# A hybrid decoder layer on one core: feed-forward features in two halves, the residual stream in DRAM during the mixer, five buffers of split weights, loads of small vectors apart from their use

## The chip, the cores and the metric

The kernel runs on one core of a Trainium2 chip. The metric is device microseconds for one execution of the whole program, as a median of several runs. Beside the timed runs one execution was profiled; its span goes from the first to the last instruction, and every trace row below is from that execution.

## The reference

One decoder layer on x, 256 positions by 2048 features, float32:

```
x = x + 0.5 * swiglu(rms_norm(x, ffn1_norm), ffn1_w_gate, ffn1_w_up, ffn1_w_down)     # 2048 -> 5632 -> 2048
h = rms_norm(x, mix_norm)
proj = h @ w_in                                        # 2048 -> 11776: q, k, v of two attentions, two gates
dq, dk = rope(rms_norm(q)), rope(rms_norm(k))          # per head, 128 wide
o_dil  = dilated attention, 3 head groups x 4 heads, mixed over the groups
o_diff = differential attention, 4 heads: softmax1 - lambda * softmax2, with a norm per head
         lambda = exp(sum(lq1 * lk1)) - exp(sum(lq2 * lk2)) + lam_init
y = sigmoid(g_dil) * (o_dil @ w_dil_branch) + sigmoid(g_diff) * (o_diff @ w_diff_branch)
x = x + y @ w_out
x = x + 0.5 * swiglu(rms_norm(x, ffn2_norm), ffn2_w_gate, ffn2_w_up, ffn2_w_down)

swiglu(h) = (silu(h @ w_gate) * (h @ w_up)) @ w_down
```

## The kernel before, in words

**Every large product goes through `linear` (L99).** It makes a block of 512 output columns for all 256 positions: two tiles of 128 positions (`NT`), each with a PSUM bank of its own. The weights come in groups of two blocks of 128 rows (`GRP`, 512 KB a group). For a group, `weight_groups` (L83) loads the raw float32 rows on SP's queue (`raw`, pool `wraw`, four buffers), ScalarE rounds them to the matmul's type (`w_hi`, L95), and VectorE takes the rest (`w_lo`, L96); these two tiles are in pool `wspl`, with three buffers of each. TensorE then does three products for each block of rows and each position tile: high by high (L111), high by low (L112), low by high (L113). So a group is 12 matmuls of 512 columns. There are 768 groups in the program: 176 for gate and up and 88 for down in each feed-forward, 184 for `w_in`, 24 for the two branches, 32 for `w_out`. A buffer of `w_hi` and `w_lo` comes free when TensorE has finished the group that read it.

**The clock of the program text is the group.** `tick` (L73) counts groups; `defer(n, fn)` (L70) puts a piece of work into the program text n groups later. The order on each engine is then made by the planner of the framework, which plays the program through with its own durations and lets each engine take what is ready, earlier text first; a load without anything to wait for can so move far ahead of its place in the text. On the chip every engine and every queue goes through its list strictly in that order and waits where something is late. `pinned` (L357 to L360) keeps what ScalarE and VectorE do in a deferred piece behind the newest split.

**Feed-forward (`ffn`, L231).** For each of 11 chunks of 512 features: gate (8 groups), SiLU, up (8 groups), product on VectorE (L247). The chunk is then turned so that features lie on partitions: `turn_blocks` (L149) transposes 32 by 32 blocks on VectorE (L155), writes them to DRAM (`blocks`, L157) and reads them back in another order (`moved`, L160), both on SP's queue. Eight groups later in the text (`BLOCK_WAIT`) `split_blocks` (L163) splits the block into `ah` (ScalarE, L128) and `al` (VectorE, L129). After all 11 chunks come four blocks of down, each of 22 groups over all 44 blocks of features. The block of the last chunk is read by groups 21 and 22 of the first of them. In the first feed-forward each finished block goes through `residual` (L254: added to `xs`, turned, split into `xh` and `xl` for the next product), in the second through `finish` (L660: added to `xs` and stored).

**The mixer** takes `w_in` in 23 blocks, with the attention heads as deferred pieces between the groups. `sig` (L597) holds the first gate, 16 KB a partition, last read by `dil_part` (L625) of the fourth block of the branches. `xs`, the residual stream (L184, 16 KB a partition), lies in SBUF throughout; the mixer only uses it in the `residual` of `w_out`.

**Small vectors.** `rotary` (L301) loads the positions on ScalarE's queue and makes the tables at once; `head_gains` (L333) loads eight vectors of 128 on ScalarE's queue, each broadcast to all partitions (64 KB), and makes lambda from four of them at once (`lq`, L338 to L346).

Of the kernel before, what the change touches and what calls it, by code (L numbers as in the profile page):

```python
# [27 lines left out]
LEAD = 56  # L28
BLOCK_WAIT = 8
GRP = 2  # L30
DIL_G, DIL_H = 3, 4
DIFF_H = 4
ROPE = 32
# [15 lines left out]
def hybrid_layer_kernel(ctx: ExitStack, tc: tile.TileContext, a: dict, out: bass.AP):  # L49
# [1 line left out]

    const = ctx.enter_context(tc.tile_pool(name="const", bufs=1))
    small = ctx.enter_context(tc.tile_pool(name="small", bufs=4))
    wraw = ctx.enter_context(tc.tile_pool(name="wraw", bufs=4))
    wspl = ctx.enter_context(tc.tile_pool(name="wspl", bufs=3))
    work = ctx.enter_context(tc.tile_pool(name="work", bufs=1))
    dram = ctx.enter_context(tc.tile_pool(name="dram", bufs=2, space=bass.MemoryType.DRAM))
    ps_mm = ctx.enter_context(tc.tile_pool(name="ps_mm", bufs=4, space=PSUM))
# [122 lines left out]
        return tot  # L181


    xs = const.tile([P, NT, D], F32, name="xs")  # L184
    xv = a["x"][0].rearrange("(t p) d -> p t d", p=P)
    ident = const.tile([P, P], F32, name="ident")
    make_identity(nc, ident)
# [43 lines left out]
    def ffn(wg, wu, wd, norm, done, ahead=None):  # L231
        with tc.tile_pool(name="act", bufs=1) as apool, tc.tile_pool(name="actw", bufs=2) as aw, \
                tc.tile_pool(name="actb", bufs=1) as bp:
            ah = apool.tile([P, KF, S], F32R, name="ah")
            al = apool.tile([P, KF, S], F32R, name="al")
            for j in range(FF // CH):
                ps = linear(wg, j * CH, xh, xl, KD, ahead if j == 0 else None)
                if j == 0:
                    rs = norm()
                sg = []  # L240
                for t in range(NT):
                    s = aw.tile([P, CH], F32, name="sg")
                    nc.scalar.activation(s, ps[t], AF.Silu, scale=rs[t])  # L243
                    sg.append(s)
                ps = linear(wu, j * CH, xh, xl, KD)
                for t in range(NT):
                    nc.vector.scalar_tensor_tensor(sg[t], ps[t], rs[t], sg[t], op0=ALU.mult, op1=ALU.mult)  # L247
                x = turn_blocks(sg, bp)
                defer(BLOCK_WAIT, lambda x=x, j=j: split_blocks(x, ah, al, 4 * j))
            for n in range(D // CH):  # L250
                ps = linear(wd, n * CH, ah, al, KF)
                done(n, ps, bp)

    def residual(n, ps, scale, gains, ss, pool):  # L254

        cols = slice(n * CH, (n + 1) * CH)
        for t in range(NT):
            nc.vector.scalar_tensor_tensor(xs[:, t, cols], ps[t], scale, xs[:, t, cols],
                                           op0=ALU.mult, op1=ALU.add)
        src = [xs[:, t, cols] for t in range(NT)]  # L260

        def turn():
            x = turn_blocks(src, pool)
            defer(BLOCK_WAIT, lambda: split_blocks(x, xh, xl, 4 * n, gains))

        def squares():
            for t in range(NT):
                sum_squares(ss[t], n, src[t])

        if n < D // CH - 1:  # L270
            defer(1, turn)
        else:
            defer(2, lambda: to_kmajor(src, xh, xl, 4 * n, gains))
        defer(3, squares)
# [25 lines left out]

    def rotary():  # L301

        pos = const.tile([P, NT], I32, name="pos")
        with nc.allow_non_contiguous_dma(reason="256 positions"):
            nc.scalar.dma_start(pos, a["positions"].rearrange("b (t p) -> p (b t)", p=P))
        posf = const.tile([P, NT], F32, name="posf")
        nc.vector.tensor_copy(posf, pos)
        freq = const.tile([P, H], F32, name="freq")
        for i, f in enumerate(INV_FREQ):
            nc.vector.memset(freq[:, i:i + 1], f)  # L310
        ang = const.tile([P, NT, H], F32, name="ang")
        turns = const.tile([P, NT, H], F32, name="turns")
        for t in range(NT):
            nc.vector.tensor_scalar(ang[:, t], freq, posf[:, t:t + 1], None, op0=ALU.mult)
        nc.vector.tensor_scalar(turns, ang, 1.0 / (2.0 * math.pi), MAGIC, op0=ALU.mult, op1=ALU.add)
        nc.vector.tensor_scalar(turns, turns, -MAGIC, None, op0=ALU.add)
        for part in (*TWO_PI, TWO_PI_REST):
            nc.vector.scalar_tensor_tensor(ang, turns, -part, ang, op0=ALU.mult, op1=ALU.add)
        aabs = turns
        nc.vector.scalar_tensor_tensor(aabs, ang, -1.0, ang, op0=ALU.mult, op1=ALU.max)  # L320
        hpi = const.tile([P, 1], F32, name="hpi")
        nc.vector.memset(hpi, math.pi / 2.0)
        sh = const.tile([P, NT, H], F32, name="sh")
        chf = const.tile([P, NT, H], F32, name="chf")
        nc.scalar.activation(sh, ang, AF.Sin, scale=0.5)
        nc.scalar.activation(chf, aabs, AF.Sin, scale=-0.5, bias=hpi)
        nc.vector.scalar_tensor_tensor(sinb[:, :, H:], sh, 2.0, chf, op0=ALU.mult, op1=ALU.mult)
        nc.vector.tensor_scalar(sinb[:, :, :H], sinb[:, :, H:], -1.0, None, op0=ALU.mult)
        nc.vector.tensor_tensor(sh, sh, sh, op=ALU.mult)
        for i in range(2):  # L330
            nc.vector.tensor_scalar(cosb[:, :, i * H:(i + 1) * H], sh, -2.0, 1.0, op0=ALU.mult, op1=ALU.add)

    def head_gains():  # L333

        for i, n in enumerate(("dil_q_norm", "dil_k_norm", "diff_q_norm", "diff_k_norm")):
            nc.scalar.dma_start(qkg[:, i], a[n].to_broadcast([P, P]))
        lq = work.tile([P, 4, P], F32, name="junk")
        for i, n in enumerate(("diff_lq1", "diff_lk1", "diff_lq2", "diff_lk2")):  # L338
            nc.scalar.dma_start(lq[:, i], a[n].to_broadcast([P, P]))
        le = const.tile([P, 2], F32, name="le")  # L340
        for i in range(2):
            nc.vector.tensor_tensor(lq[:, 2 * i], lq[:, 2 * i], lq[:, 2 * i + 1], op=ALU.mult)
# [16 lines left out]
    def pinned(fn):  # L359

        with tc.issue_after(last_hi.ins), tc.issue_after(last_lo.ins):
            fn()

    defer(28, lambda: pinned(masks))
    defer(36, lambda: pinned(rotary))
    defer(44, lambda: pinned(head_gains))
    ss = [small.tile([P, D // CH], F32, name="ss4") for _ in range(NT)]
    ffn(a["ffn1_w_gate"][0], a["ffn1_w_up"][0], a["ffn1_w_down"][0], first_norm,
        lambda n, ps, pool: residual(n, ps, 0.5, later_gains[0], ss, pool), lambda g: load_x(g + 1))


    rstd = []
# [2 lines left out]
    o_dq, o_dk, o_dv = 0, 1536, 3072  # L375
    o_fq, o_fk, o_fv = 4608, 5632, 6656
    o_ga, o_gb = 7680, 9728

    mix = ExitStack()
    midc = mix.enter_context(tc.tile_pool(name="midc", bufs=1))  # L380
# [6 lines left out]
    ob_h = midc.tile([P, 2 * DIFF_H, S], F32R, name="ob_h")  # L387
    ob_l = midc.tile([P, 2 * DIFF_H, S], F32R, name="ob_l")

    def qk_chunk(c0, gain, dst, is_key):  # L390


        ps = linear(w_in, c0, xh, xl, KD)
        if not rstd:
            rstd.extend(rsqrt_mean(total(mix_ss[t]), D, 1) for t in range(NT))
        q = midw.tile([P, NT, 4, P], F32, name="q")
# [55 lines left out]
    fk = fp.tile([P, 2, 4, NT, 4, 32], F32, name="fk")  # L452
    fv = fp.tile([P, NT, 2 * P * DIFF_H], F32, name="fv")
    for i in range(2):
        qk_chunk(o_fq + i * CH, 2, fq[:, 4 * i:4 * i + 4], False)
        qk_chunk(o_fk + i * CH, 3, fk[:, i], True)
        v_chunk(o_fv + i * CH, fv, i * CH)

# [156 lines left out]
    for n in range(D // CH):  # L615
# [29 lines left out]

        defer(2, turn_y)
    gpool.__exit__(None, None, None)
    ss = [small.tile([P, D // CH], F32, name="ss4") for _ in range(NT)]
    for n in range(D // CH):
        ps = linear(a["w_out"][0], n * CH, yh, yl, KD)  # L650
# [45 lines left out]
```

## Time and profile before

| | |
|---|---|
| time, median of 3 runs | 2173.26 us (2169.95 to 2179.61) |
| time of the profiled execution | 2174.9 us |
| its span | 2173.1 us |
| mean granted TensorE clock | 0.998 |
| TensorE busy | 2148.0 us (99%) |
| VectorE busy | 1216.5 us (56%) |
| ScalarE busy | 994.6 us (46%) |
| GpSimd busy | 45.1 us (2%) |
| DMA, mean | 208 GB/s |

1.8 us of the profiled execution lie outside its span. A busy TensorE is not one at its peak: the end of a matmul is modelled, and consecutive matmuls overlap, so the distance from start to start says more than the busy share.

### The profile page before, as it was taken

What the parts mean: (1) busy time and instruction counts of PE and PEld (TensorE: products, weight loads), DVE (VectorE), ACT (ScalarE), POOL (GpSimd) and SP (SyncE); (2) the same over time, 40 slices, a digit from 0 to 9 for tenths busy, and PEclk for the clock granted to TensorE, in tenths of its full rate; (3) what the DMA queues carried; (4) which work ended last, traced back from release to release, by engine and by line L of the source; (5) the groups of instructions that cost most, each with busy time, mean ns of one, the idle gap of its engine ahead of it and who ended that gap; (6) DMA issues with size and microseconds to landing.
All of it is one profiled execution on the core that took longest, in us unless ns stands there. A gap on an engine that the chain in (4) does not pass through costs nothing.

```text
span 2173.1 us, 24998 instructions
## 1 busy us (share of the span) xinstructions
PE 2148.0 (99%) x9490; PEld 1765.7 (81%) x9490; DVE 1216.5 (56%) x1440; ACT 994.6 (46%) x1193; POOL 45.1 (2%) x41
## 2 busy tenths in 40 slices
PE   8999999999999999999999999999999999999999
PEld 7878888888888877887878888888888888888887
DVE  5655555555555466776565556665555555554443
ACT  5434444443444445555455444454444444443333
POOL 0000000000000010101100000000000000000000
PEclk9999999999999999999999999999999999999999
DMA  6666666666666666666654566666666666666654
GB/s 231 211 201 215 218 213 221 220 217 210 209 210 199 198 202 204 205 221 208 208 190 159 184 226 214 218 214 213 213 218 210 223 212 212 224 216 207 203 203 141
DMA packets 241437, 452.04 MB, mean 208 GB/s; under 512 B 14322, under 2 KB 38436, under 8 KB 241316
## 3 DMA queue, kind: packets, MB, share of 16 engines
q1 hardware_dynamic: 239792, 449.89, 63.1%
q8 instruction: 74, 1.21, 0.2%
q10 hardware_dynamic: 1524, 0.55, 0.1%
q14 instruction: 47, 0.39, 0.0%
HBM read 426.80 MB, written 23.59 MB: 207 GB/s over the span
## 4 chain that ended last, share of the span: by engine, by line
PE 79%; DMA 10%; DVE 6%; ACT 2%; issue 2%; POOL 1%; SPq 0%; ACTq 0%; DVEq 0%; POOLq 0%
PE mm L112 26%; PE mm L113 26%; PE mm L111 26%; DMA moved<-blocks 4%; DMA blocks<-turned 4%; DVE w_lo L96 3%; ACT w_hi L95 2%; DVE turned L155 1%; POOL rr L122 1%; DMA q<-blocks 1%; DMA raw<-in_w_out_dram 1%; DMA raw<-in_ffn_w_up_dram 0%; DVE q L407 0%; PE s L552 0%; DMA dk<-blocks 0%
## 5 line engine op out<-in xcount | busy, mean ns | idle before, releaser
L96 DVE TENSOR_TENSOR w_lo<-raw,w_hi 128x1024 fp32r<-128x1024 f32 (+1 forms) x769 | 933.0, 1220 | 793.7 <-ACT w_hi L95 792.8
L95 ACT ACTIVATE w_hi<-raw 128x1024 fp32r<-128x1024 f32 (+1 forms) x769 | 808.8, 1058 | 949.5 <-PE mm L113 919.7
L112 PE MATMUL mm<-w_lo,xh 128*128 128x512 f32 x2144 | 843.1, 393 | 8.4 <-DVE w_lo L96 7.9
L113 PE MATMUL mm<-w_hi,xl 128*128 128x512 f32 x2144 | 834.5, 390 | 0.1
L111 PE MATMUL mm<-w_hi,xh 128*128 128x512 f32 x2144 | 759.3, 392 | 0.1
L112 PEld LDWEIGHTS mm<-w_lo,xh 128*128 128x128 f32 x2144 | 403.8, 188 | 99.6 <-DVE w_lo L96 16.6
L111 PEld LDWEIGHTS mm<-w_hi,xh 128*128 128x128 f32 x2144 | 403.0, 188 | 85.6 <-ACT w_hi L95 1.6
L113 PEld LDWEIGHTS mm<-w_hi,xl 128*128 128x128 f32 x2144 | 403.5, 188 | 83.1 <-DVE xl L132 0.5
L112 PE MATMUL mm<-w_lo,ah 128*128 128x512 f32 x704 | 274.5, 390 | 2.6 <-DVE w_lo L96 2.6
L113 PE MATMUL mm<-w_hi,al 128*128 128x512 f32 x704 | 274.0, 389 | 0.0
L111 PE MATMUL mm<-w_hi,ah 128*128 128x512 f32 x704 | 245.7, 389 | 0.1
L112 PEld LDWEIGHTS mm<-w_lo,ah 128*128 128x128 f32 x704 | 132.2, 188 | 32.2 <-DVE w_lo L96 4.7
L111 PEld LDWEIGHTS mm<-w_hi,ah 128*128 128x128 f32 x704 | 131.8, 188 | 28.6 <-ACT w_hi L95 1.1
L113 PEld LDWEIGHTS mm<-w_hi,al 128*128 128x128 f32 x704 | 132.1, 188 | 27.2
L122 POOL TENSOR_TENSOR rr<-rv,mhalf 128x4 f32<-128x4 f32 (+1 forms) x34 | 44.2, 1306 | 1404.6 <-DVE rv L120 1404.5
L129 DVE TENSOR_TENSOR al<-moved,ah 128x512 fp32r<-128x512 f32 x44 | 28.5, 688 | 73.0 <-ACT ah L128 73.0
L128 ACT ACTIVATE ah<-moved 128x512 fp32r<-128x512 f32 x44 | 25.4, 624 | 86.4 <-DMA moved<-blocks 86.4
L112 PE MATMUL mm<-w_lo,yh 128*128 128x512 f32 x128 | 50.2, 392 | 0.7 <-DVE w_lo L96 0.7
L113 PE MATMUL mm<-w_hi,yl 128*128 128x512 f32 x128 | 49.9, 390 | 0.0
L155 DVE STREAM_TRANSPOSE turned<-sg 128x512 f32<-128x512 f32 x44 | 48.4, 1100 | 0.0
L111 PE MATMUL mm<-w_hi,yh 128*128 128x512 f32 x128 | 44.9, 390 | 0.1
L243 ACT ACTIVATE sg<-mm,rr 128x512 f32<-128x512 f32 x44 | 29.8, 689 | 21.5 <-PE mm L113 21.5
(142 smaller groups left out, 733.4 us busy)
## 6 DMA issues: line engine op xcount, KB each, us to landing
raw<-in_w_in_dram SPq DMA_DIRECT2D x184, 512.0 KB, 3.5
raw<-in_ffn_w_up_dram SPq DMA_DIRECT2D x176, 512.0 KB, 4.5
raw<-in_ffn_w_down_dram SPq DMA_DIRECT2D x176, 512.0 KB, 4.4
raw<-in_ffn_w_gate_dram SPq DMA_DIRECT2D x175, 512.0 KB, 4.0
blocks<-turned SPq DMA_DIRECT2D x41, 512.0 KB, 4.4
raw<-in_w_out_dram SPq DMA_DIRECT2D x32, 512.0 KB, 4.5
moved<-blocks SPq DMA_DIRECT2D x31, 512.0 KB, 4.5
raw<-in_w_diff_branch_dram SPq DMA_DIRECT2D x16, 512.0 KB, 4.7
```

The source lines that it names most:

```text
L95: last_hi = nc.scalar.activation(hi[:, ks], raw[:, ks], AF.Copy)
L96: last_lo = nc.vector.tensor_tensor(lo[:, ks], raw[:, ks], hi[:, ks].bitcast(F32), op=ALU.subtract)
L111: nc.tensor.matmul(ps[t], xh[:, k, sl], hi[:, kk], start=k == 0, stop=False)
L112: nc.tensor.matmul(ps[t], xh[:, k, sl], lo[:, kk], start=False, stop=False)
L113: nc.tensor.matmul(ps[t], xl[:, k, sl], hi[:, kk], start=False, stop=k == nk - 1)
L122: nc.gpsimd.tensor_tensor(r, v, mhalf[:, :cols], op=ALU.pow)
L128: nc.scalar.activation(hi, src, AF.Copy)
L129: nc.vector.tensor_tensor(lo, src, hi.bitcast(F32), op=ALU.subtract)
L155: nc.vector.transpose(r[:, :, t], srcs[t].rearrange("p (kt i q) -> p q kt i", i=32, q=4))
L243: nc.scalar.activation(s, ps[t], AF.Silu, scale=rs[t])
```

## The change

- Pool `wspl` gets five buffers of `w_hi` and `w_lo` instead of three; `wraw` stays at four.
- `ffn` does the features in two halves of 6 and 5 chunks. After the first half come four blocks of down of 12 groups, whose results `part` adds to `xs`; after the second half four blocks of 10 groups, with `residual` or `finish` as before. `ah` and `al` are 24 blocks long instead of 44.
- `xs` moves into a pool of its own at the right end of SBUF. In the first feed-forward `residual` also stores each finished block to DRAM (`x_mid`). The first product of the mixer is pulled ahead of the closing of that pool; the mixer's tiles use its place. Before `w_out`, in the place of `sig`, a new `xs` is loaded from `x_mid` in one transfer of 2 MB on SP's queue.
- The loads of the positions and of the eight small vectors move from ScalarE's queue into `table_loads`, on GpSimd's queue, at group 34 of the text and not pinned. `rotary` moves from group 36 to 40, `head_gains` from 44 to 48.

```diff
+RAW_BUFS = 4
+SPL_BUFS = 5
+HALVES = (6, 5)
...
-    wraw = ctx.enter_context(tc.tile_pool(name="wraw", bufs=4))
-    wspl = ctx.enter_context(tc.tile_pool(name="wspl", bufs=3))
+    wraw = ctx.enter_context(tc.tile_pool(name="wraw", bufs=RAW_BUFS))
+    wspl = ctx.enter_context(tc.tile_pool(name="wspl", bufs=SPL_BUFS))
...
-    xs = const.tile([P, NT, D], F32, name="xs")
+    xpool = tc.tile_pool(name="xpool", bufs=1, side="right")
+    xs = xpool.__enter__().tile([P, NT, D], F32, name="xs")
+    x_mid = dram.tile([NT, P, D], F32, name="x_mid", bufs=1)
...
-            ah = apool.tile([P, KF, S], F32R, name="ah")
-            al = apool.tile([P, KF, S], F32R, name="al")
-            for j in range(FF // CH):
...
+            ah = apool.tile([P, 4 * HALVES[0], S], F32R, name="ah")
+            al = apool.tile([P, 4 * HALVES[0], S], F32R, name="al")
+            rs = None
+            j = 0
+            for half, count in enumerate(HALVES):
+                down = wd[j * CH:(j + count) * CH]
+                for i in range(count):
+                    ps = linear(wg, j * CH, xh, xl, KD, ahead if j == 0 else None)
...
+                    x = turn_blocks(sg, bp)
+                    defer(BLOCK_WAIT, lambda x=x, i=i: split_blocks(x, ah, al, 4 * i))
+                    j += 1
+                for n in range(D // CH):
+                    ps = linear(down, n * CH, ah, al, 4 * count)
+                    (done if half else part)(n, ps, bp)
+
+    def part(n, ps, _):
+        cols = slice(n * CH, (n + 1) * CH)
+        for t in range(NT):
+            nc.vector.scalar_tensor_tensor(xs[:, t, cols], ps[t], 0.5, xs[:, t, cols], op0=ALU.mult, op1=ALU.add)
...
+        if keep is not None:
+            nc.sync.dma_start(keep.rearrange("t p d -> p t d")[:, :, cols], xs[:, :, cols])
...
-        pos = const.tile([P, NT], I32, name="pos")
-        with nc.allow_non_contiguous_dma(reason="256 positions"):
-            nc.scalar.dma_start(pos, a["positions"].rearrange("b (t p) -> p (b t)", p=P))
...
-    def head_gains():
+    def table_loads():
 
         for i, n in enumerate(("dil_q_norm", "dil_k_norm", "diff_q_norm", "diff_k_norm")):
-            nc.scalar.dma_start(qkg[:, i], a[n].to_broadcast([P, P]))
+            nc.gpsimd.dma_start(qkg[:, i], a[n].to_broadcast([P, P]))
         lq = work.tile([P, 4, P], F32, name="junk")
         for i, n in enumerate(("diff_lq1", "diff_lk1", "diff_lq2", "diff_lk2")):
-            nc.scalar.dma_start(lq[:, i], a[n].to_broadcast([P, P]))
+            nc.gpsimd.dma_start(lq[:, i], a[n].to_broadcast([P, P]))
+        lam_in.append(lq)
+        with nc.allow_non_contiguous_dma(reason="256 positions"):
+            nc.gpsimd.dma_start(pos, a["positions"].rearrange("b (t p) -> p (b t)", p=P))
+
+    def head_gains():
+        lq = lam_in[0]
...
+    defer(34, table_loads)
     defer(28, lambda: pinned(masks))
-    defer(36, lambda: pinned(rotary))
-    defer(44, lambda: pinned(head_gains))
+    defer(40, lambda: pinned(rotary))
+    defer(48, lambda: pinned(head_gains))
...
-        lambda n, ps, pool: residual(n, ps, 0.5, later_gains[0], ss, pool), lambda g: load_x(g + 1))
+        lambda n, ps, pool: residual(n, ps, 0.5, later_gains[0], ss, pool, x_mid), lambda g: load_x(g + 1))
...
+    first = linear(w_in, o_fq, xh, xl, KD)
+    xpool.__exit__(None, None, None)
...
-        qk_chunk(o_fq + i * CH, 2, fq[:, 4 * i:4 * i + 4], False)
+        qk_chunk(o_fq + i * CH, 2, fq[:, 4 * i:4 * i + 4], False, None if i else first)
...
     gpool.__exit__(None, None, None)
+    xpool = ctx.enter_context(tc.tile_pool(name="xpool2", bufs=1, side="right"))
+    xs = xpool.tile([P, NT, D], F32, name="xs")
+    nc.sync.dma_start(xs, x_mid.rearrange("t p d -> p t d"))
```

## Rows read from the trace of the kernel before

**Rows 1.** The page: busy time of each engine; shares of the chain that ended last.

```profile
PE 2148.0 (99%) x9490; PEld 1765.7 (81%) x9490; DVE 1216.5 (56%) x1440; ACT 994.6 (46%) x1193; POOL 45.1 (2%) x41
...
PE 79%; DMA 10%; DVE 6%; ACT 2%; issue 2%; POOL 1%; SPq 0%; ACTq 0%; DVEq 0%; POOLq 0%
```

**Rows 2.** Waits of TensorE: waited for, us in total, times, longest us.

```profile
PE mm L112 <- DVE w_lo L96: 11.2, 16, 3.5
...
PE s L552 <- DMA dk<-blocks: 2.0, 2, 1.0
```

**Rows 3.** Timeline of a steady stretch: start us, us, engine, line, operation.

```profile
582.27 0.62 PE L111 MATMUL mm<-w_hi,ah 128*128 128x512 f32 x2
582.47 1.06 ACT L95 ACTIVATE w_hi<-raw 128x1024 fp32r<-128x1024 f32 x1 [1.67 <-PE mm L113]
583.57 1.23 DVE L96 TENSOR_TENSOR w_lo<-raw,w_hi 128x1024 fp32r<-128x1024 f32 x1 [1.50 <-ACT w_hi L95]
...
585.00 0.62 PE L111 MATMUL mm<-w_hi,ah 128*128 128x512 f32 x2
```

**Rows 4.** Timeline at the first block of down; brackets: idle before, and its end.

```profile
501.44 1.40 DVE L247 SCALAR_TENSOR_TENSOR sg<-mm,rr,sg 128x512 f32<-128x512 f32 x2
...
510.62 0.37 SPq L160 DMA_DIRECT2D moved<-blocks  x1
...
515.82 1.16 ACT L128 ACTIVATE ah<-moved 128x512 fp32r<-128x512 f32 x2 [4.68 <-DMA moved<-blocks]
516.88 2.94 ACT L95 ACTIVATE w_hi<-raw 128x1024 fp32r<-128x1024 f32 x3
...
516.49 1.29 DVE L129 TENSOR_TENSOR al<-moved,ah 128x512 fp32r<-128x512 f32 x2 [4.09 <-ACT ah L128]
...
518.04 0.67 PE L111 MATMUL mm<-w_hi,ah 128*128 128x512 f32 x2
519.24 0.50 PE L112 MATMUL mm<-w_lo,ah 128*128 128x512 f32 x1 [0.53 <-DVE w_lo L96]
519.57 0.39 PE L113 MATMUL mm<-w_hi,al 128*128 128x512 f32 x1
```

**Rows 5.** Timeline around `head_gains`; last row a stretch, its third figure the granted clock.

```profile
133.09 0.33 ACTq L339 DMA_DIRECT2D junk<-in_diff_lk_dram  x1
133.53 2.01 ACT L95 ACTIVATE w_hi<-raw 128x1024 fp32r<-128x1024 f32 x2 [5.12 <-DMA junk<-in_diff_lq_dram]
...
136.69 0.29 DVE L342 TENSOR_TENSOR junk<-junk 128x128 f32<-128x128 f32 x1 [7.03 <-DMA junk<-in_diff_lk_dram]
...
138.13 1.22 DVE L96 TENSOR_TENSOR w_lo<-raw,w_hi 128x1024 fp32r<-128x1024 f32 x1
...
135.31 0.61 PE L111 MATMUL mm<-w_hi,xh 128*128 128x512 f32 x2
139.41 0.79 PE L112 MATMUL mm<-w_lo,xh 128*128 128x512 f32 x1 [3.48 <-DVE w_lo L96]
...
144.69 0.46 PE L112 MATMUL mm<-w_lo,xh 128*128 128x512 f32 x1
...
142.00:144.00 2.00, 2.00 (x6) 0.50 0.82 267
```

**Rows 6.** The start: a stretch (last three: clock, DMA share, GB/s), timeline, one DMA issue.

```profile
4.00:22.00 18.00, 16.38 (x71) 13.27 (x71) 11.03 (x17) 9.82 (x16) 0.00 (x0) 1.00 1.01 348
...
1.30 0.39 ACTq L200 DMA_DIRECT2D g_raw<-in_mix_norm_dram  x1
...
35.66 0.24 POOL L290 IOTA junk<- 128x128 int32 x1
...
qkg<-in_dil_q_norm_dram ACTq DMA_DIRECT2D x1, 64.0 KB, 4.1
```

**Rows 7.** Timeline before and in `w_out`; last row from the groups by line.

```profile
1345.32 1.28 DVE L627 TENSOR_TENSOR y<-mm,sig 128x512 f32<-128x512 f32 x2
...
1378.85 1.28 DVE L258 SCALAR_TENSOR_TENSOR xs<-mm,xs 128x512 f32<-128x512 f32 x2
...
L258 DVE SCALAR_TENSOR_TENSOR xs<-mm,xs 128x512 f32<-128x512 f32 x16 | 10.2, 681 | 0.0
```

More of the change, by code (lines that the diff above doesn't have):

```diff
@@ L233, in ffn @@
                 tc.tile_pool(name="actb", bufs=1) as bp:
-            ah = apool.tile([P, KF, S], F32R, name="ah")
-            al = apool.tile([P, KF, S], F32R, name="al")
-            for j in range(FF // CH):
[L237 to L254, printed above, removed]
+            ah = apool.tile([P, 4 * HALVES[0], S], F32R, name="ah")
[6 more added lines that the diff above has]
+                    ps = linear(wg, j * CH, xh, xl, KD, ahead if j == 0 else None)
+                    if rs is None:
+                        rs = norm()
+                    sg = []
+                    for t in range(NT):
+                        s = aw.tile([P, CH], F32, name="sg")
+                        nc.scalar.activation(s, ps[t], AF.Silu, scale=rs[t])
+                        sg.append(s)
+                    ps = linear(wu, j * CH, xh, xl, KD)
+                    for t in range(NT):
+                        nc.vector.scalar_tensor_tensor(sg[t], ps[t], rs[t], sg[t], op0=ALU.mult, op1=ALU.mult)
+                    x = turn_blocks(sg, bp)
[4 more added lines that the diff above has]
+                    (done if half else part)(n, ps, bp)
@@ L256, in residual @@
+    def part(n, ps, _):
+        cols = slice(n * CH, (n + 1) * CH)
+        for t in range(NT):
+            nc.vector.scalar_tensor_tensor(xs[:, t, cols], ps[t], 0.5, xs[:, t, cols], op0=ALU.mult, op1=ALU.add)
+    def residual(n, ps, scale, gains, ss, pool, keep=None):
         cols = slice(n * CH, (n + 1) * CH)
@@ L331, in rotary @@
             nc.vector.tensor_scalar(cosb[:, :, i * H:(i + 1) * H], sh, -2.0, 1.0, op0=ALU.mult, op1=ALU.add)
-    def head_gains():
+    pos = const.tile([P, NT], I32, name="pos")
+    lam_in = []
+    def table_loads():
         for i, n in enumerate(("dil_q_norm", "dil_k_norm", "diff_q_norm", "diff_k_norm")):
-            nc.scalar.dma_start(qkg[:, i], a[n].to_broadcast([P, P]))
+            nc.gpsimd.dma_start(qkg[:, i], a[n].to_broadcast([P, P]))
         lq = work.tile([P, 4, P], F32, name="junk")
         for i, n in enumerate(("diff_lq1", "diff_lk1", "diff_lq2", "diff_lk2")):
-            nc.scalar.dma_start(lq[:, i], a[n].to_broadcast([P, P]))
+            nc.gpsimd.dma_start(lq[:, i], a[n].to_broadcast([P, P]))
[4 more added lines that the diff above has]
+        lq = lam_in[0]
         le = const.tile([P, 2], F32, name="le")
@@ L388, in hybrid_layer_kernel, with qk_chunk @@
     ob_l = midc.tile([P, 2 * DIFF_H, S], F32R, name="ob_l")
-    def qk_chunk(c0, gain, dst, is_key):
-        ps = linear(w_in, c0, xh, xl, KD)
+    def qk_chunk(c0, gain, dst, is_key, ps=None):
+        ps = ps or linear(w_in, c0, xh, xl, KD)
         if not rstd:
```

## The prediction, as it was put on record

> **What bounds the kernel now.** I read the page first: TensorE is busy 99% of the span, and the chain that ended last runs 79% over it [rows 1]. So every other engine matters only through what it makes TensorE wait for. The change removes no matmul: 176 groups of gate and up and 4 x (12 + 10) = 88 groups of down are as many as before. A steady stretch gives the price of a group: its double L111 starts at 582.27 and the next at 585.00 us, 12 matmuls in about 2.72 us, 0.227 us each [rows 3]. 768 groups then take 2089 us, which neither kernel can go below; of the 2173.1 us of span only 84 us are anything else, and most of that is the heads' small matmuls, the start and the end. I look for TensorE's waits inside those 84 us.
>
> The waits of TensorE name one cause far ahead of the rest: the low half of a split weight, `w_lo`, 16 times, 11.2 us in total, the longest 3.5 us [rows 2]. The other waits of the middle are small (2.0 us for `dk`, for instance).
>
> Why `w_lo` is late is in the timeline. In the steady stretch ScalarE starts `w_hi` right when TensorE leaves the group whose buffer it takes, and `w_lo` is done 582.47 to 584.80, 2.33 us after it [rows 3]. With three buffers the split of a group so starts two groups before its use, 5.44 us ahead; the slack is 5.44 - 2.33 = 3.1 us. Anything that holds ScalarE or VectorE longer stops TensorE. At the seam to the down blocks it is the turned features: ScalarE's list has the split of `moved` ahead of the next `w_hi`, the transfer was only issued at 510.62, and ScalarE sits idle 4.68 us for it. The next three `w_hi` then run in one piece, so their raw weights had long been there, and TensorE waits at 519.24 [rows 4]. Around `head_gains` it is the small vectors: ScalarE issues their loads, the last at 133.09, while its next `w_hi` has to stand behind; VectorE waits 7.03 us for them to land, with `w_lo` queued behind that wait, and TensorE gets it at 139.41. It then runs at half clock (2.4 GHz down to 1.2) until about 144.7: 6 matmuls in a stretch of 2 us with a granted clock of 0.50 [rows 5].
>
> **The change, part by part.**
>
> *Five buffers.* The split starts four groups ahead instead of two: 10.88 - 2.33 = 8.55 us of slack. The holds seen are 4 to 5 us at a seam [rows 4] and 7.0 us at the vectors [rows 5]. All are under 8.55, so every wait for `w_lo` should go. What they cost: 16 waits are 11.2 us [rows 2]; without the longest, 15 are 7.7 us. That counts only idle after a modelled end. From start to start, the double L111 at 518.04 should be followed after 0.45 us, and is after 1.20 (0.75 lost); the next step takes 0.33 instead of 0.227 (0.10 lost) [rows 4]. So a wait booked as 0.53 costs 0.85, or 0.32 more. 15 waits: 7.7 + 15 x 0.32 = 12.5 us. Bounds: 7.7 if the booked time is all, 15 if some small waits that no row names go with them. I take 12.5, because it is measured from starts.
>
> Raw weights keep four buffers, so they could become the limit. A raw buffer is free when `w_lo` of four groups before is done, so a load is issued 10.88 - 2.33 = 8.55 us ahead of its `w_hi`, with three split buffers as with five: it moves ahead together with the splits.
>
> *Loads apart from use.* The ninth load is issued about 30 us or more before its use instead of just ahead of it. The wait goes: the pair at 135.31 to 139.41 should take 0.45 and takes 4.10 (3.65 lost), and the 13 matmuls from there to 145.0 us take 5.6 us where 13 x 0.227 = 2.95 would do (2.6 lost) [rows 5]. Sum 6.3 us. The five buffers would hide most of that wait alone (7.0 is under 8.55), so the two edits share it; it is counted once. Its bounds are 5 and 6.3.
>
> GpSimd has nothing of weight to do then (45.1 us in the whole span) [rows 1]. Not being pinned, the loads of the norms need nothing and will move to the start, as the load at 1.30 us did, though its text stands at group 20; the index table on GpSimd also ran at 35.66 instead of about 76 us [rows 6]. There the DMA engines are full: share 1.01 at 348 GB/s from 4 to 22 us. Four loads of 64 KB are 0.26 MB, 0.75 us at that rate [rows 6]. I charge 0.75 us to the start; bounds 0 (TensorE isn't waiting for each byte there) and 1.5 (small rows, twice the price). The other four need the buffer that the masks use and come at about 90 us, 40 us before `head_gains`.
>
> *Halves.* Eight more pairs of adds, `part`, in each feed-forward's first half are 4 x 1.28 us on VectorE each [rows 7], which has 44% idle [rows 1]; a pair delays a `w_lo` by 1.28 us, inside the 8.55 (and inside the old 3.1, were that cover gone). The PSUM banks alternate, and the next block of 10 or 12 groups takes at least 27 us. So: nothing. The seams get tighter. The last turned block was read by group 21 of 22; now it is by group 11 of 12 or group 9 of 10. From the first add after up at 501.44 to the end of the split at 517.78 are 16.3 us, 6.0 groups [rows 4]; group 9 starts 8 groups, 21.8 us, after up. 5.4 us remain: nothing, with a rival below.
>
> *xs in DRAM.* Four stores of 512 KB behind `residual`, on SP's queue. The store waits for the same add that the turning after it waits for, so raw loads behind it are held a little over a microsecond; no charge. The load back can be issued when `dil_part` has read `sig` for the last time, at 1345.32 + 1.28 = 1346.6 us, and `xs` is first used at 1378.85 [rows 7]. 2.1 MB at 348 GB/s take 6.0 us [rows 6], of 32 us that there are; raw loads behind it come up to 6.0 us late, hidden by the 8.55. If that cover were gone (three buffers), TensorE would stop for about 6.0 - 3.1 = 2.9 us. Pulling the first product ahead of the pool's closing adds no instruction.
>
> **Sum.** 2174.9 - 12.5 - 6.3 + 0.75 = 2156.9 us on the profiled execution, 18 us or 0.8% less. That execution is 1.6 us above the median of the three runs, so the median lies a little lower: 2156. What a measurement can tell here is about 0.5%, 10.9 us from 2173.26: at or below 2162.4 is faster.
>
> **The rivals.**
>
> *The extra buffers bring no lead.* If raw weights are the true limit, the splits can't run further ahead and the 12.5 us stay: 2174.9 - 6.3 + 0.75 = 2169.3, no change. For it: SP stands still from a block's store to its reload at each seam, and raw loads queue behind that. Against: three `w_hi` in one piece after the hold [rows 4] had their raw tiles waiting. Chance 0.12.
>
> *The table loads on GpSimd land late.* The wait of VectorE then comes back; beyond 8.55 us it stops TensorE one for one, with some 2.6 us for the clock [rows 5]. A wait of 14 us gives 2156.9 + 5.5 + 2.6 = 2165, no change. It needs loads issued near 90 us to be on their way for over 50 us, where the same loads on ScalarE's queue took 4.1 [rows 6]. For it speaks the Trainium skill, "SBUF — State Buffer", section "SBUF: two separate sides": GpSimd writes the descriptors of its own DMAs, and can't while VectorE runs an operation in its two-port mode. No GpSimd DMA is in this trace to agree or not. Chance 0.03. Partial successes of about the same time, 0.03.
>
> *Slower: the seams.* A hold at one place: the split of the last block before group 9 of the second half, or group 11 of the first. It decides from 21.8 us after up; now it takes 16.3. Each microsecond beyond stops TensorE, plus 2.6 us for the clock once it is long. There are four seams of halves; to be slower by 10.9 us they must eat the 18 us first: (18 + 10.9) / 4 = 7.2 us each, a split 26 to 29 us after up. Time then 2185 us. For it: the list of ScalarE is fixed by the planner, and it may put `w_hi` of later groups, which wait for TensorE, ahead of the split. Against: before, it put the split too early, not too late [rows 4]. Chance 0.04.
>
> **How the numbers follow.** My forecast, waits for `w_lo` gone, has 0.78, with 2151 to 2162: 2.5 us more from small waits and 1.5 us from the `dk` wait and a free start at the low end, the bounds 7.7 and 5 at the other. Faster 0.78, the two cases of no change and the partial ones 0.18, slower 0.04. The range reaches to the late-load case and holds some of the no-change ones: 2151 to 2166.
>
> **What the profile would show.** Right: hardly a wait of TensorE for `w_lo`; ScalarE still idle 4 to 5 us ahead of `ah`; clock 1.00 from 130 to 150 us; `qkg` loads in the first microseconds. Wrong, if the waits for `w_lo` stay, if they now name raw loads, or if a seam's L112 or L113 waits for `ah` or `al`. What I hold least sure is the planner: with other buffers it makes another order on every engine, and a new wait of a few microseconds could come from any of them.

## The result, and the profile after

The changed kernel takes 2147.65 us (median of 4 runs, 2147.51 to 2147.96), the kernel before 2172.44 us beside it (4 runs, 2169.95 to 2179.61): a ratio of 0.9872, 95% interval 0.9855 to 0.9889. It is faster, as forecast, but by 24.8 us where 18 were forecast, and 3.4 us below the range of 2151 to 2166. The profiled execution takes 2147.71 us, its span is 2145.9 us.

The page of the kernel after, the two lines that answer to [rows 1]:

```profile
PE 2133.2 (99%) x9490; PEld 1766.7 (82%) x9490; DVE 1226.7 (57%) x1456; ACT 993.5 (46%) x1193; POOL 47.7 (2%) x50
...
PE 99%; DMA 0%; DVE 0%; SPq 0%; issue 0%
```

The same matmuls make up 99% of the chain now, where other engines held 21% of it. All waits of TensorE of the kernel after, against [rows 2]:

```profile
PE tr L144 <- DMA xs<-in_x_dram: 4.5, 2, 4.3
PE tr L210 <- DMA g_raw<-in_ffn_norm_dram: 3.9, 1, 3.9
```

Both are in the first 10 us; no wait for `w_lo`, `dk` or anything else is left. The seam to the first block of down, which now stands after six chunks, in the timeline (against [rows 4]):

```profile
275.61 1.40 DVE L258 SCALAR_TENSOR_TENSOR sg<-mm,rr,sg 128x512 f32<-128x512 f32 x2
...
288.36 0.39 PE L115 MATMUL mm<-w_lo,ah 128*128 128x512 f32 x1
...
288.59 0.39 PE L116 MATMUL mm<-w_hi,al 128*128 128x512 f32 x1
...
289.98 1.15 ACT L131 ACTIVATE ah<-moved 128x512 fp32r<-128x512 f32 x2 [4.66 <-DMA moved<-blocks]
...
290.64 1.29 DVE L132 TENSOR_TENSOR al<-moved,ah 128x512 fp32r<-128x512 f32 x2 [4.07 <-ACT ah L131]
...
291.04 2.94 ACT L98 ACTIVATE w_hi<-raw 128x1024 fp32r<-128x1024 f32 x3
```

The hold is the old one: ScalarE idle 4.66 us for `moved`, then three `w_hi` in one piece. TensorE goes on at 0.23 us a matmul through it. From the first product after up on VectorE (L258; the prediction calls it an add) to the end of `al` at 291.93 are 16.3 us, as before.

Where the time went shows in the length of each stage, from the first 512-column matmul of one to that of the next (worked out from the timeline of TensorE, us; the second feed-forward is counted to the start of its last matmul):

| stage | before | after | |
|---|---|---|---|
| start | 7.5 | 10.5 | +2.9 |
| first feed-forward | 737.6 | 722.4 | -15.2 |
| `w_in` with the heads | 480.4 | 471.0 | -9.4 |
| branches | 131.0 | 130.5 | -0.5 |
| `w_out` | 89.7 | 88.0 | -1.7 |
| second feed-forward | 722.1 | 718.75 | -3.4 |
| end | 4.8 | 4.7 | |

The second feed-forward is at its floor: 264 groups of 2.72 us are 718.1.

### The profile page after: what moved, and what is told of

Read it like the earlier page. It is cut to its first block, busy times and chain, and to the rows that moved or that the text cites. A ratio compares the mean times of both kernels' runs of the same rounds, so it can differ in the third digit from the quotient of the medians.

```text
span 2145.9 us, 25034 instructions
## 1 busy us (share of the span) xinstructions
PE 2133.2 (99%) x9490; PEld 1766.7 (82%) x9490; DVE 1226.7 (57%) x1456; ACT 993.5 (46%) x1193; POOL 47.7 (2%) x50
## 4 chain that ended last, share of the span: by engine, by line
PE 99%; DMA 0%; DVE 0%; SPq 0%; issue 0%
PE mm L114 33%; PE mm L115 32%; PE mm L116 32%; PE s L581 0%; DMA xs<-in_x_dram 0%; PE tr L144 0%; PE s L500 0%; PE tr L610 0%; PE s L534 0%; PE tr L599 0%; PE tr L611 0%; PE tr L547 0%; DVE xs L695 0%; PE tr L522 0%; SPq L96 0%; SPq L225 0%
## 5 line engine op out<-in xcount | busy, mean ns | idle before, releaser
L114 PE MATMUL mm<-w_hi,xh 128*128 128x512 f32 x2144 | 837.0, 391 | 0.0
L114 PE MATMUL mm<-w_hi,ah 128*128 128x512 f32 x704 | 273.9, 389 | 0.0
L131 ACT ACTIVATE ah<-moved 128x512 fp32r<-128x512 f32 x44 | 25.4, 624 | 89.3 <-DMA moved<-blocks 89.3
L114 PE MATMUL mm<-w_hi,yh 128*128 128x512 f32 x128 | 49.9, 390 | 0.0
```

What stands on the lines that cost most here:

```text
L114: nc.tensor.matmul(ps[t], xh[:, k, sl], hi[:, kk], start=k == 0, stop=False)
L131: nc.scalar.activation(hi, src, AF.Copy)
```

## The experiments

Each is the changed kernel with the edit shown, or the kernel before where the text says so. Ratios are to the kernel before on the same chip.

**How many buffers.** Three and four buffers of split weights in place of five.

```diff
-SPL_BUFS = 5
+SPL_BUFS = 3      # three_bufs; four_bufs: 4
```

> The changed kernel with three buffers of split weights instead of five; halves, residual stream in DRAM and loads apart stay. Theory A (the lead of the splits carries the gain): the slack falls from 8.55 to 3.1 us, the waits of TensorE for w_lo come back at the seams and in the heads, 15 to 20 of them at about 1 us, and with them the waits of the scores for dk; the half clock around 140 us does not come back, since the loads stay apart. 2147.7 + 15 to 22 = 2163 to 2170 us. Rival B (the gain came from the planner's new order around the halves and the moved residual stream, the lead is spare): at most 5 us more, 2148 to 2153 us.

> The changed kernel with four buffers of split weights: the split starts three groups ahead, slack 8.16 - 2.33 = 5.8 us. Theory A: the holds of 4 to 5 us at the seams fit, longer ones in the heads do not quite; within 3 us of the changed kernel, 2147 to 2151 us. Rival C (each buffer gives the same): half of what three buffers lose comes back, about 2156 to 2159 us. Rival B: as with five, 2148 us.

Three: 2173.47 us (10 runs, 2168.37 to 2177.12), ratio 0.999 (0.9978 to 1.0002) (2163 to 2170 us were expected). Four: 2148.07 us, 0.988 (0.9866 to 0.9895). So the whole gain hangs on the step from three to four, 25.4 us (23.9 between the profiled spans), and the fifth buffer adds nothing that can be measured. Without the buffers all other parts together are worth nothing that can be measured. The waits of TensorE's matmuls and weight loads with three buffers:

```profile
PE mm L115 <- DVE w_lo L99: 7.6, 15, 0.8
...
PE s L581 <- DMA dk<-blocks: 2.7, 2, 1.4
PE mm L114 <- ACT w_hi L98: 1.3, 4, 0.4
PE s L500 <- DMA fk<-blocks: 1.1, 1, 1.1
```

```profile
PEld mm L115 <- DVE w_lo L99: 19.7, 30, 1.3
PEld mm L114 <- ACT w_hi L98: 4.7, 9, 0.9
```

With four, one row of 0.2 us for `w_lo` is left at the weight loads and none at the matmuls. With three, the matmul rows add up to 12.7 us of the 23.9, the two rows of weight loads alone to 24.4; this gap is taken up below.

**The other parts by themselves.** The kernel before with the halves alone; the kernel before with the loads apart alone; features whole, with four split and, for room, three raw buffers; and three split buffers with six raw ones.

```diff
# halves_only, loads_only: the kernel before with only that part of the change
# whole_four_three_raw
-RAW_BUFS = 4
-SPL_BUFS = 5
-HALVES = (6, 5)
+RAW_BUFS = 3
+SPL_BUFS = 4
+HALVES = (11,)
# three_split_six_raw
-RAW_BUFS = 4
-SPL_BUFS = 5
+RAW_BUFS = 6
+SPL_BUFS = 3
```

> The kernel before with the feed-forward features in two halves alone: three buffers, residual stream in SBUF, loads at their use. Theory A: no gain of its own; two more seams in each feed-forward, each worth about a microsecond of waiting for w_lo at three buffers: 0 to 4 us more than the kernel before. Rival B (the new order of the halves carries the gain): 10 us less or more.

> The kernel before with the loads of small vectors apart from their use alone. By the terms measured so far: the wait and the half clock around 135 to 145 us go (6.3 us), the start gets 2 to 3 us longer since the loads go out in the first microseconds: 3 to 4 us less than the kernel before of the same chip, within what can be told. Rival (the loads are the larger half of the result): 10 us less or more.

> The changed kernel with the features whole again (11 chunks, then four blocks of down of 22 groups), four buffers of split weights, and three of raw weights, which makes the room for it. Theory A: the halves only make room; the lead of three groups is there, so 2148 us, at most 3 us more because a raw load is issued only 5.8 us ahead of its split. Rival B (halves needed for the gain): 2160 us or more. Rival H (raw weights are the true limit): three raw buffers bring the waits back, 2165 us or more.

> The changed kernel with three buffers of split weights and six of raw weights: the 8 KB of one pair of split buffers spent on two raw buffers. Theory A: raw weights are not what is late, so as with three split and four raw: 2170 to 2175 us, no change from the kernel before. Rival H (any deeper queue of weights does it): 2148 to 2155 us.

| | us | ratio |
|---|---|---|
| halves alone | 2174.62 | 0.9997 (0.9982 to 1.0012) |
| loads apart alone | 2170.49 | 0.9981 (0.9965 to 0.9998) |
| whole, four split, three raw | 2152.29 | 0.9889 (0.9867 to 0.9911) |
| three split, six raw | 2174.17 | 0.9996 (0.9979 to 1.0013) |

The halves and the residual stream in DRAM only make room. More raw weights in place of split ones bring nothing, and one raw buffer fewer leaves nearly the whole gain: the split, not the load, was what came late.

**The loads of the vectors.** Back on ScalarE's queue at their use, with five and with four buffers; and, on GpSimd, held back behind the two powers of the first norm.

```diff
# loads_at_use, four_at_use (with SPL_BUFS = 4)
-            nc.gpsimd.dma_start(qkg[:, i], a[n].to_broadcast([P, P]))
+            nc.scalar.dma_start(qkg[:, i], a[n].to_broadcast([P, P]))
...
-    defer(48, lambda: pinned(head_gains))
+    defer(48, lambda: pinned(lambda: (table_loads(), head_gains())))
# loads_held
+    def held_loads():
+        with tc.issue_after(last_pow.ins):
+            table_loads()
```

> The changed kernel with the loads of the small vectors put back on ScalarE's queue, directly ahead of their use, five buffers kept. Theory F (the five buffers hide that wait alone: VectorE's hold of about 7 us is under the slack of 8.55): VectorE waits for the vectors again, TensorE hardly, clock 1.00 throughout, and the start is shorter by 2.9 us: 2144 to 2147 us. Rival G (the loads apart carry their 6.3 us whatever the buffers): the wait and the half clock come back, 2147.7 + 6.3 - 2.9 = 2151 us.

> The changed kernel with four buffers of split weights and the loads of small vectors back on ScalarE's queue directly ahead of their use: the one hold that is longer than the slack of four buffers (7.0 us against 5.8). Theory A (a hold costs what it exceeds the slack by): one wait of TensorE for w_lo of about 1 to 1.5 us around 135 us and no half clock: 1 to 2 us more than five buffers with the loads at use (2145.9). Rival (the hold is hidden with four as with five): the same as with five, no wait of TensorE for w_lo. Rival (the wait of 3.5 us with its half clock comes back): 6 us more.

> The changed kernel with one edit: the loads of the small vectors on GpSimd's queue are held behind the two powers of the first norm, at about 38 us, so that none of them is issued in the first microseconds. Theory D (their transfers delay the second piece of x, on which TensorE waits 4.3 us at the start): the start gets 2.5 to 3 us shorter, 2144.5 to 2145.5 us. Rival E (the start is longer because ScalarE's order there is another): no change, 2147 to 2148 us.

At use, five buffers: 2145.86 us, 0.9869 (0.9855 to 0.9884). At use, four: 2147.87 us, 0.9871 (0.9857 to 0.9886). Held: 2146.03 us, 0.9869 (0.9855 to 0.9884). In the timeline of VectorE with the loads at their use and five buffers the old wait is there again:

```profile
131.16 1.23 DVE L99 TENSOR_TENSOR w_lo<-raw,w_hi 128x1024 fp32r<-128x1024 f32 x1 [1.45 <-ACT w_hi L98]
139.28 0.29 DVE L369 TENSOR_TENSOR junk<-junk 128x128 f32<-128x128 f32 x1 [6.89 <-DMA junk<-in_diff_lk_dram]
```

6.89 us ([rows 5]: 7.03), and TensorE doesn't wait; the granted clock from 130 to 150 us is 1.00. Once the splits run ahead, the loads apart from their use are worth nothing, and where they stand now they cost the start. With four buffers the wait of VectorE was 7.11 us, and TensorE didn't wait there either: its two waits for `w_lo` (1.2 us in all) were elsewhere, so the expectation was right in size by luck and wrong in place. Counted with the limit that the holds below measured (4.33 us with three buffers, one group more with four: 7.05) this wait was to cost TensorE nothing.

The start of the kernel after, in the timeline:

```profile
1.29 0.71 POOL L355 DMA_DIRECT2D qkg<-in_dil_q_norm_dram  x1 [0.34 <-issue]
...
9.73 1.08 PE L144 MATMUL tr<-ident,xs 128*128 128x128 f32 x4 [4.34 <-DMA xs<-in_x_dram]
...
10.46 0.77 PE L114 MATMUL mm<-w_hi,xh 128*128 128x512 f32 x1
```

The `qkg` loads moved to the first microseconds, as expected of loads that nothing holds. The load of `x` that TensorE waits for is issued when it was before (2.21 us; before, 2.20), but it lands later. Its row in the list of DMA issues, with the time to landing last, after and before:

```profile
xs<-in_x_dram SPq DMA_DIRECT2D x1, 256.0 KB, 7.4
```

```profile
xs<-in_x_dram SPq DMA_DIRECT2D x1, 256.0 KB, 4.5
```

These 2.9 us are those by which TensorE's first 512-column matmul came later, at 10.46 instead of 7.54 us. Held back, the `qkg` loads leave it at 7.55 us, yet only 1.6 us of the 2.9 come off the time: the stage behind the start grows from 722.4 to 723.7 us. There TensorE's weight loads now wait three times, about 0.5 us each, for the split of later pieces of `x` (`xh`, `xl`), between 16 and 18.5 us.

**The order of the scores.** Three buffers, but the score matmuls of the heads tied behind the newest weight matmul of the text.

```diff
-SPL_BUFS = 5
+SPL_BUFS = 3
...
-        return (0, lambda: scores(0)), (2, lambda: scores(1)), (5, turn), (7, values), (10, turn_out)
+        return (0, lambda: behind(lambda: scores(0))), (2, lambda: behind(lambda: scores(1))), (5, turn), (7, values), (10, turn_out)
# behind(fn): with tc.issue_after(last_mm.ins): fn()
```

> The changed kernel with three buffers of split weights, and the score matmuls of all heads tied behind the newest weight matmul of their place in the text, so that the planner can't pull single ones forward. Theory P (at three buffers the planner sees TensorE idle, fills the idle time with score matmuls whose keys land later on the chip than it reckons, and TensorE then waits for dk and fk): these waits, 3.8 us in the run with three buffers, go; the waits for w_lo stay: about 4 us less than three buffers, 2169 us. Rival (the waits come from the late keys whatever the order): the waits for dk and fk stay, no change.

2168.16 us, ratio 0.9971 (0.9954 to 0.9989). The dilated scores in the timelines of TensorE, with three buffers and then tied:

```profile
1025.03 0.49 PE L581 MATMUL s<-dk,dq 128*128 128x128 f32 x2 [1.34 <-DMA dk<-blocks]
...
1094.20 0.49 PE L581 MATMUL s<-dk,dq 128*128 128x128 f32 x2 [1.40 <-DMA dk<-blocks]
```

```profile
1096.25 0.83 PE L588 MATMUL s<-dk,dq 128*128 128x128 f32 x6
```

With three buffers the order on TensorE has pairs of score matmuls in front of weight matmuls, and on the chip they wait for their keys. (Presumably TensorE has gaps in the planner's own run then, and it fills them with what it thinks ready; the planner's times were not seen.) Tied, six stand together and none waits; the stage with the heads falls from 480.0 to 477.1 us. That the waits go is shown by these rows; what they are worth in the whole program is less sure. The two intervals overlap, and the profiled execution of the tied kernel took 2173.76 us, the longest of its nine, with longer waits for `w_lo` than the untied one (10.7 us at the matmuls against 7.6). With five buffers the planner itself puts them together, six at 1080.04 us.

**Artificial holds.** To test the law of the slack directly (TensorE loses what a hold exceeds the slack by), one VectorE instruction of growing length, whose result is not used, stands at five places of the first feed-forward, with five and with three buffers (loads held in both).

```diff
+    def hold(count):
+        j = work.tile([P, CH], F32, name="junk")
+        nc.vector.memset(j, 1.0)
+        m = small.tile([P, 1], F32, name="held")
+        nc.vector.tensor_reduce(m, j[:, None, :].to_broadcast([P, count, CH]), axis=AX.XY, op=ALU.max)
+
+    for at, count in ((74, 9), (90, 13), (154, 18), (170, 22), (186, 27)):
+        defer(at, lambda count=count: pinned(lambda: hold(count)))
```

> Five split buffers, with one artificial VectorE instruction of growing length (9, 13, 18, 22 and 27 x 512 elements) put into the list at five places of the first feed-forward, away from the seams; the output does not use it. At about 0.55 us for 512 elements (worked out from w_lo, 1024 in 1.22 us, less its fixed part) the holds are about 5, 7, 10, 12 and 15 us. Theory (slack 8.55 us): VectorE has 1.5 us free per group, so the next w_lo is late by the hold less 1.5; TensorE loses what exceeds 8.55: 0, 0, 0, about 2 and about 5 us, with up to 2.6 more for the clock at the last. Rival (the raw weights limit the lead, so five buffers give no more slack than three): TensorE loses 0.4, 2.6, 5.3, 7.5 and 10 us.

> The same with three split buffers. Theory (slack 5.44 - 2.33 = 3.1 us): TensorE loses the hold less 1.5 and less 3.1: about 0.4, 2.6, 5.3, 7.5 and 10 us, with up to 2.6 more each for the clock where the wait is long. Rival (the count of buffers is not what sets the slack): the losses are those of the run with five.

One execution each: spans of 2191.9 and 2230.7 us, against 2144.3 with the loads held and no holds, and 2169.7 with three buffers. The waits of TensorE for `w_lo` are only 7.5 and 29.3 us of that. The rest was something else: every matmul with `xh` or `xl` took 0.2324 us or more from start to start instead of 0.2267, in both feed-forwards and in `w_in`, also where no hold is. The new tile `held` lies ahead of the weights: in the built programs `w_hi` begins at 77344 instead of 77216, and `xh` stays at 17088. So the holds were repeated with the result in an old tile, and the shift was made alone.

```diff
# holds_five_same_place, holds_three_same_place
-        nc.vector.tensor_reduce(m, j[:, None, :].to_broadcast([P, count, CH]), axis=AX.XY, op=ALU.max)
+        nc.vector.tensor_reduce(j[:, 480:481], j[:, None, :480].to_broadcast([P, count, 480]), axis=AX.XY, op=ALU.max)
# weights_shifted: the changed kernel, and
+    gap = small.tile([P, 1], F32, name="gap")
+    nc.vector.memset(gap, 0.0)
```

> Holds as in holds_five, of about 5.2, 7.3, 9.8, 11.8 and 14.9 us, the result kept in an old tile, so that no tile moves. Theory (slack 8.55 us; lateness is the hold less the 1.5 us that VectorE has free): TensorE loses 0, 0, 0, 1.8 and 4.9 us, with up to 2.6 for the clock at the last ones; span about 2144.3 + 7 + 4 = 2152 to 2156, and a pitch of 0.227 us throughout. Rival (the holds themselves slow the matmuls): the pitch stays at 0.232 and the span near 2192.

> The same with three split buffers. Theory (slack 3.1 us): losses of about 0.6, 2.7, 5.2, 7.2 and 10.3 us, 26 in all, and up to 2.6 each for the clock in the last four; against the span of three buffers without holds (2169.7, less 1.6 for the start) about 2194 to 2204. Rival (the matmuls are slowed by the holds): near 2231.

> The changed kernel with one more small tile, which is written once and not used, in the pool that lies ahead of the weights: every weight buffer moves by 128 bytes against xh and xl, and ah, al, yh and yl move with the weights. Theory (the distance between the operands of a matmul sets its pitch): matmuls with xh and xl take about 0.2324 us instead of 0.2267, 6432 of them, some 37 us more: about 2185 us. Rival (the holds did it, not the place): 2148 us, as the changed kernel.

Spans of 2161.3 and 2207.3 us, with the old pitch; both lie above what was expected (2152 to 2156 and 2194 to 2204). With three buffers each hold is followed by a wait; in the timeline of TensorE, the first four of the five:

```profile
216.76 0.50 PE L116 MATMUL mm<-w_lo,xh 128*128 128x512 f32 x1 [0.66 <-DVE w_lo L100]
...
263.60 0.73 PE L116 MATMUL mm<-w_lo,xh 128*128 128x512 f32 x1 [2.65 <-DVE w_lo L100]
...
444.73 0.80 PE L116 MATMUL mm<-w_lo,xh 128*128 128x512 f32 x1 [5.16 <-DVE w_lo L100]
...
497.22 0.80 PE L116 MATMUL mm<-w_lo,xh 128*128 128x512 f32 x1 [7.16 <-DVE w_lo L100]
```

The forecasts count the slack and the 1.5 us that VectorE has free in a group (3.1 + 1.5 and 8.55 + 1.5):

| hold, us | lost, three buffers | forecast (hold - 4.6) | lost, five buffers | forecast (hold - 10.05) |
|---|---|---|---|---|
| 5.15 | 0.82 | 0.55 | 0 | 0 |
| 7.15 | 2.82 | 2.55 | 0 | 0 |
| 9.65 | 5.32 | 5.05 | 0 | 0 |
| 11.65 | 7.32 | 7.05 | 4.62 | 1.6 |
| 14.65 | 10.33 | 10.05 | 7.42 | 4.6 |

Lost is counted from start to start of the matmuls, without the clock, which takes some 1.5 to 2.8 us more after all but the shortest loss (with three buffers the granted clock is 0.50 from 264 to 267 us, behind the second hold). With three buffers the law holds to 0.3 us: hold less 4.33. With five the first three cost nothing. The last two cost 3 us too much, about a group, and the lists of VectorE and ScalarE show why, here for the first of the two:

```profile
463.18 1.15 ACT L133 ACTIVATE ah<-moved 128x512 fp32r<-128x512 f32 x2 [4.94 <-DMA moved<-blocks]
...
468.25 11.65 DVE L400 TENSOR_REDUCE junk<-junk 128x1 f32<-128x11040 f32 x1
479.82 4.62 DVE L100 TENSOR_TENSOR w_lo<-raw,w_hi 128x1024 fp32r<-128x1024 f32 x4
```

The hold began 4 us after the hold of a seam, before the splits had won their lead back; the last one stands the same way, with `al` at 513.54 and the hold at 517.94 us. The third, which cost nothing, came after four `w_lo` at an even 2.72 us. Lateness adds up while the lead is not full. So with five buffers no hold over 9.65 us met a full lead, and that a loss begins at 10.05 us is not shown.

The shift alone: 2184.3 us (5 runs, 2184.11 to 2184.62), ratio 1.0042 (1.0028 to 1.0056). Two stretches of 20 us away from the heads, of the shifted kernel and then of the kernel after (PE busy and matmuls, PEld, DVE, ACT, POOL, granted clock, DMA share, GB/s):

```profile
40.00:60.00 20.00, 20.00 (x88) 16.21 (x87) 11.20 (x11) 9.24 (x10) 0.00 (x0) 1.00 0.60 190
500.00:520.00 20.00, 20.00 (x88) 16.22 (x87) 13.06 (x14) 8.65 (x10) 0.00 (x0) 1.00 0.67 219
```

```profile
40.00:60.00 20.00, 20.00 (x90) 16.57 (x89) 11.62 (x12) 9.08 (x10) 0.00 (x0) 1.00 0.64 200
500.00:520.00 20.00, 20.00 (x90) 16.55 (x89) 10.42 (x10) 9.81 (x12) 0.00 (x0) 1.00 0.70 237
```

88 matmuls instead of 90 at full clock and with no wait: 6432 matmuls x 0.0057 us (0.2324 less 0.2267) = 36.7 us, which is the difference of 36.65 us.

## Why the prediction was wrong in size, and right in its cause

**Five buffers: the cause was right, the size wrong.** This is the term that failed. It was put at 12.5 us, bounds 7.7 and 15; the spans with three and four buffers differ by 23.9 (the medians by 25.4), and the stages come near it: 27.2 us saved, plus the 1.6 to 2.9 given up at the start, less 6.3 at `head_gains`, are 22.5 to 23.8. The working started from TensorE's matmul rows, 16 waits of 11.2 us. Those rows begin at the modelled end of the matmul before: in the holds each wait is booked 0.16 us below its start-to-start loss (0.66 for 0.82, 10.16 for 10.33), so a short one leaves little or no idle time and stands in no row. Taken from start to start over the whole trace (a 512-column matmul at 0.2267 us), the kernel before loses:

| steps | before | after |
|---|---|---|
| over 0.5 us late, matmul to matmul | 15, 14.5 us | 0 |
| 0.06 to 0.5 us late, matmul to matmul | 126, 18.1 us | 65, 7.7 us |
| matmul to a score, over 0.5 us late | 3, 3.7 us | 0 |

The 15 large ones are 10.8 us without the 3.65 at `head_gains`: the forecast had these right. What it didn't have are the many small ones, 10.4 us of difference, of which 2.6 are the clock after `head_gains` and the 0.10 us after each of 15 waits was in the sum: some 6 us. And 3.7 us of scores, which it left in place ("1.5 us from the `dk` wait" at the low end only); that they go is a doing of the planner's order, shown by the run with the scores tied. Together 10 of the missing 11.4 us. The runs with three and four buffers, which differ in this one number of the text, close the rest: counted the same way, 11.4 us of large steps against none, 15.3 of small ones against 7.9 and 4.3 before scores against none make 23.2 of the 23.9 us. The planner makes another order for each count of buffers; what that is worth beyond the scores was not separated. The view that would have warned is the same list of waits for the weight loads, which the prediction did not read. Of the kernel before:

```profile
PEld mm L112 <- DVE w_lo L96: 23.0, 28, 3.9
...
PEld mm L111 <- ACT w_hi L95: 3.2, 8, 0.5
PEld s L552 <- DMA dk<-blocks: 2.9, 2, 1.4
...
PEld s L471 <- issue: 1.6, 1, 1.6
```

30.7 us in all, 26.8 without `head_gains`; with four buffers 0.2 us of it is left. It is somewhat too much, since a load in time would also have stood still a little, but nearer 23.9 than 11.2 is.

**The slack.** 3.1 us was right to 0.3 us, and nothing speaks against 8.55: the artificial holds lost what the law says with three buffers, and nothing up to 9.65 us with five, where the slack of four buffers would have covered 7.05. The law has one more clause: it counts from a full lead.

**Loads apart: 6.3 us were there, and were shared as said.** Alone in the kernel before they took 4 us off, the 6.3 less some 2 at the start. In the changed kernel they take nothing off, because the lead covers the 7 us. The sum counted the gain once and stays right. Granted clock of the kernel after around `head_gains`, against the 0.50 in [rows 5]:

```profile
130.00:150.00 20.00, 20.00 (x90) 16.57 (x89) 13.28 (x18) 9.24 (x10) 0.00 (x0) 1.00 0.62 191
```

**The start: charged 0.75, bounds 0 and 1.5; it was 2.9, of which 1.6 to 1.8 can be had back.** The charge took the loads as bytes at the stretch's rate. What came late was one load of `x`, by 2.9 us at the same time of issue; why it is held up by so much more than the bytes is open, and that small rows cost twice their bytes, the upper bound of the charge, no run shows. The two runs without these loads at the start show 7.1 and 7.55 us to the first large matmul.

**The rivals.** That the buffers bring no lead fell: no wait of TensorE names raw loads, and more raw buffers did nothing. With the longer lead ScalarE, though, does wait for raw weights, which it hardly did before (2.7 us, 3 times, all told); of the kernel after, the largest row:

```profile
ACT w_hi L98 <- DMA raw<-in_w_in_dram: 25.7, 17, 3.0
```

These waits cost TensorE nothing.

GpSimd's loads were not late: the list of DMA issues gives the time to landing in its last column.

```profile
junk<-in_diff_lk_dram POOLq DMA_DIRECT2D x2, 64.0 KB, 4.9
...
qkg<-in_diff_q_norm_dram POOLq DMA_DIRECT2D x1, 64.0 KB, 7.2
```

That is 5 us for a load before `head_gains`, as it was on ScalarE's queue (5.3 and 4.7), and 7 at the crowded start, the longest of the eight. The rule of the Trainium skill, "SBUF — State Buffer", section "SBUF: two separate sides", that VectorE in its two-port mode can keep GpSimd from writing its descriptors, left no mark that can be seen here. The seams did not get too late: 16.3 us in the first half and 15.6 (623.77 to 639.34) in the second, with group 9 at 21.8.

**Halves and `xs` in DRAM: nothing, as forecast.** The reload took longer than the 6.0 us estimated. Its issue, with the last reader of `sig`, whose place it takes (L656), and its first use (L275), from the timelines of SP and VectorE of the kernel after:

```profile
1323.28 1.28 DVE L656 TENSOR_TENSOR y<-mm,sig 128x512 f32<-128x512 f32 x2
...
1324.58 0.37 SPq L679 DMA_DIRECT2D xs<-x_mid  x1
...
1356.82 1.28 DVE L275 SCALAR_TENSOR_TENSOR xs<-mm,xs 128x512 f32<-128x512 f32 x2
```

It lands after 10.7 us, of the 32 that there are, and no wait names it; for the raw loads of `w_out` behind it ScalarE waits twice, 0.8 us in all, and TensorE never.

**A better version** than the change follows: with the loads back at their use 2145.86 us, or held back 2146.03, against 2147.65. Four buffers would do (2148.07), which leaves 8 KB a partition free.

## What to carry to other kernels

A buffer count is a time: so many groups of lead, less the work from free to ready. Put every hold of the feeding engines beside it, add holds that follow each other before the lead is won back, and one buffer more is worth all of what exceeds it; past that it is worth nothing. Read the waits of the weight loads beside those of the matmuls, or count from start to start, because many short waits are not booked. And when an experiment adds a tile, look at the pitch of the matmuls before believing its time.

## What the runs showed that was not expected

**The place of the tiles is worth 36.65 us.** 128 bytes between the weights and `xh` made each of their matmuls 2.5% slower; `ah`, `al`, `yh` and `yl`, which moved along with the weights, kept 0.2267 us. Before and after the change the distance from `xh` to the first `w_hi` is the same 60128 bytes, so the pitch is no part of the result; one small tile in the wrong pool would have made the same change measure as slower. Both kernels fix this distance with `LEAD`, 56 unused elements (224 bytes) ahead of the values of `xh`, so the values themselves are 59904 bytes from `w_hi`, 117 x 512. Which other distances are good, and why, was not tried.

**Three buffers also scatter.** The experiments with three buffers of split weights spread by 7 to 14 us from run to run (9 or 10 runs each; 2168.37 to 2177.12 with three in the changed kernel), those with four or five by 0.2 to 3 us (4 or 5 runs each; 2147.53 to 2149.27 with four). That a lead which covers the lateness also covers its changes from run to run would explain it; no run tests it.
